# Seven products of block sums for the FFN up projection, and a down projection in parts

## The chip, the cores and the metric

The kernel runs on one core of one Trainium2 chip. The metric is the device time of one execution in microseconds (us); lower is better. Engines are named as in the profile: PE (TensorE, matmul) with PEld (its weight loads), DVE (VectorE), ACT (ScalarE), POOL (GpSimd) and SP (the queue that issues most transfers).

## The reference

The input x is 512 tokens by 1024 features in float32. Two layers follow each other: a token mixer (gated linear attention in layer 0, grouped-query softmax attention in layer 1) and, after each, a gated MLP, the FFN, which this change is about:

```python
def conv_ffn(h, w_up, w_conv, b_conv, w_down):
    u = h @ w_up                       # (512, 1024) @ (1024, 5632)
    u = depthwise_conv_width3(u, w_conv) + b_conv
    val, gate = jnp.split(u, 2, axis=-1)
    return (jax.nn.silu(gate) * val) @ w_down    # (512, 2816) @ (2816, 1024)

x = x + conv_ffn(rmsnorm(x, norm_ffn[i]), ...)
```

The 2816 hidden features are 22 chunks of 128. A chunk has a value half and a gate half, each 128 features wide.

## The kernel before

**Data.** Everything lies feature by token: x is eight tiles of 128 features by 512 tokens (`x[c]`). Each float32 operand of a projection is used as two float32r pieces, high and low, and a product is three matmuls: high by high, high by low, low by high (`mm3`, lines 268 to 272).

**Weights.** The class `Weights` (line 103) keeps a list `todo` of half tiles of 128 by 1024 in the order of use. `make` loads a raw tile of 1 MB on the SP queue into one of two buffers, and makes the high piece on ACT and the low piece on DVE (`split`, lines 143 and 144), into one of three `wh` and `wl` buffers each. For a few attention weights (`by_dma`) the low piece is made without DVE: ACT writes the negated high piece (line 124), and a transfer issued by POOL adds the raw weights to it (line 133, issued at the next `flush`). `half` hands out one half and makes the next one ahead.

**FFN** (`ffn`, line 588). For each of the 22 chunks, two feature tiles (value and gate) of 8 times `mm3` with 512 tokens as moving columns go into a PSUM bank each: 48 matmuls. The input of these matmuls is x times the norm's weight. The token factor R of the norm comes later: the sum of squares is turned into R by matmuls and copies beside chunk 0 (`tokens`, `rows`, line 266), and DVE multiplies the PSUM result by R (line 605). Then the width-3 convolution on ACT and DVE (lines 607 to 609), SiLU, product and split into high and low (lines 611 to 615) give `gu`, the down projection's input. All 22 `gu` are kept. After the last chunk, the down projection runs over the eight feature tiles of the output: 22 times `mm3` into one bank, one DVE addition to x (line 633), then the pieces and squares for the next norm (`chunk`).

**Order.** The program's text gives each instruction its rank, and a planner at compile time orders each engine's queue by rank among what it reckons to be ready. An engine then works its queue strictly in that order. Tiles share buffers by tag; a new tile waits until an earlier holder's last reader is done. The tag `g` has 22 buffers of 4 KB per partition (`gu` and much else), `xhl` has 8 (the norm's pieces).

## Time and profile before

| what | value |
|---|---|
| median of 3 timed runs | 1135.24 us |
| lowest and highest | 1134.88 and 1135.59 us |
| profiled execution | span of 1132.5 us from the first to the last instruction; the page gives no time around it, and the median lies 2.74 us above the span |
| PE, share of the span | 99% busy |
| DVE | 60% |
| ACT | 42% |
| POOL | 8% |
| FFN of layer 0 | from 231 to 592 us |
| FFN of layer 1 | from 768 to 1129 us |

A busy time of one matmul is longer than the distance to the next one, since matmuls are pipelined; the cost of a run of matmuls is therefore read from the distance of their starts. A line number is that of the kernel before, and a helper's line stands for all its callers, so tiles are named with it (`up` and `dn` are the PSUM banks of the up and down projection, `av` and `po` those of two attention steps).

### The profile page before, as it was taken

The numbers are of one execution on the slowest core, as the hardware profiler recorded it, in microseconds if no ns is written. First come the engines' busy times: TensorE is split into PE (matmuls) and PEld (weight loads), VectorE is DVE, ScalarE is ACT, GpSimd is POOL, SyncE is SP. The second block draws the span as 40 slices with busy tenths as digits, with TensorE's granted clock in tenths as the row PEclk, the third lists the DMA queues.
The fourth block names the chain that finished last, engine by engine and source line by source line (L and its number), as shares of the span: only waits on it lengthen the run. The fifth ranks groups of instructions, "written<-read, shape, count | busy, mean of one in ns | idle before, by whom it ended". The sixth has DMA issues, their size and how long they took to land. (4 is left out here: it accounts for less than half of the span.)

```text
span 1132.5 us, 13117 instructions
## 1 busy us (share of the span) xinstructions
PE 1124.2 (99%) x5266; PEld 937.4 (83%) x5266; DVE 683.7 (60%) x989; ACT 481.2 (42%) x690; POOL 86.2 (8%) x74
## 2 busy tenths in 40 slices
PE   9999999999999999999999999999999999999998
PEld 7878888888888888888888888888888888888887
DVE  6576654577777777633325688766777677762221
ACT  5555233444444444422234667644444444442210
POOL 0214110000000000000004343000000000000000
PEclk9999999999999999999999999999999999999999
DMA  6322221222323223233247765423232232323320
GB/s 230 121 100 77 75 75 38 75 98 89 112 75 112 95 91 112 76 110 106 81 132 194 182 171 158 150 75 112 75 112 80 107 111 76 111 84 121 130 93 19
DMA packets 24589, 120.06 MB, mean 106 GB/s; under 512 B 2896, under 2 KB 3536, under 8 KB 13008
## 3 DMA queue, kind: packets, MB, share of 16 engines
q1 hardware_dynamic: 17328, 102.29, 26.0%
q0 software_dynamic: 2304, 8.39, 3.9%
q10 hardware_dynamic: 4896, 8.54, 2.1%
q8 instruction: 41, 0.67, 0.2%
q14 instruction: 20, 0.16, 0.0%
HBM read 100.34 MB, written 2.10 MB: 90 GB/s over the span
## 5 line engine op out<-in xcount | busy, mean ns | idle before, releaser
L143 ACT ACTIVATE wh<-raw 128x1024 fp32r<-128x1024 f32 x164 | 172.9, 1055 | 338.0 <-PE up L271 132.8
L144 DVE TENSOR_TENSOR wl<-raw,wh 128x1024 fp32r<-128x1024 f32 x164 | 203.8, 1243 | 142.7 <-ACT wh L143 142.3
L270 PE MATMUL up<-xhl,wh 128*128 128x512 f32 x704 | 274.3, 390 | 0.0
L272 PE MATMUL up<-xhl,wl 128*128 128x512 f32 x704 | 273.9, 389 | 0.0
L271 PE MATMUL up<-xhl,wh 128*128 128x512 f32 x704 | 273.9, 389 | 0.0
L271 PEld LDWEIGHTS up<-xhl,wh 128*128 128x128 f32 x704 | 132.2, 188 | 27.6
L272 PEld LDWEIGHTS up<-xhl,wl 128*128 128x128 f32 x704 | 132.1, 188 | 27.4
L270 PEld LDWEIGHTS up<-xhl,wh 128*128 128x128 f32 x704 | 132.1, 188 | 27.2
L271 PE MATMUL dn<-gu,wh 128*128 128x512 f32 x354 | 137.3, 388 | 0.0
L272 PE MATMUL dn<-gu,wl 128*128 128x512 f32 x354 | 137.3, 388 | 0.0
L270 PE MATMUL dn<-gu,wh 128*128 128x512 f32 x354 | 137.3, 388 | 0.0
L605 DVE TENSOR_TENSOR u<-up,R 128x512 f32<-128x512 f32 x88 | 60.3, 687 | 52.7 <-PE up L272 52.7
L299 PE MATMUL vg<-wh,xhl 128*128 128x512 f32 x256 | 80.1, 391 | 1.5 <-DVE halfneg L188 0.7
L607 ACT ACTIVATE y<-u,cw 128x512 f32<-128x512 f32 x88 | 71.1, 811 | 20.4 <-DVE u L605 20.4
L270 PEld LDWEIGHTS dn<-gu,wh 128*128 128x128 f32 x354 | 66.5, 188 | 13.8
L271 PEld LDWEIGHTS dn<-gu,wh 128*128 128x128 f32 x354 | 66.5, 188 | 13.7
L272 PEld LDWEIGHTS dn<-gu,wl 128*128 128x128 f32 x354 | 66.5, 188 | 13.5
L325 PE MATMUL op<-oT,wh 128*128 128x512 f32 x256 | 71.1, 394 | 0.3 <-DVE oT L710 0.3
L609 DVE SCALAR_TENSOR_TENSOR y<-u,cw,y 128x511 f32<-128x511 f32 x88 | 65.9, 751 | 2.9
L608 DVE SCALAR_TENSOR_TENSOR y<-u,cw,y 128x511 f32<-128x511 f32 x88 | 65.6, 746 | 0.6 <-ACT y L607 0.6
L611 ACT ACTIVATE y<-y 128x512 f32<-128x512 f32 x44 | 27.9, 633 | 87.8 <-DVE y L609 87.8
L299 PEld LDWEIGHTS vg<-wh,xhl 128*128 128x128 f32 x256 | 48.0, 188 | 12.4 <-DVE g L368 1.0
(187 smaller groups left out, 1432.3 us busy)
## 6 DMA issues: line engine op xcount, KB each, us to landing
raw<-in_w_up_dram SPq DMA_DIRECT2D x44, 1024.0 KB, 4.8
raw<-in_w_down_dram SPq DMA_DIRECT2D x22, 1024.0 KB, 4.8
wl<-raw POOLq DMA_DIRECT2D x16, 512.0 KB, 4.8
pr<-p ACTq DMA_DIRECT2D x32, 256.0 KB, 3.1
raw<-in_w_vg_dram SPq DMA_DIRECT2D x6, 1024.0 KB, 4.8
raw<-in_w_akq_dram SPq DMA_DIRECT2D x5, 1024.0 KB, 5.3
raw<-in_w_kq_dram SPq DMA_DIRECT2D x4, 1024.0 KB, 4.7
raw<-in_w_gout_dram SPq DMA_DIRECT2D x4, 1024.0 KB, 4.8
```

What stands on the lines that cost most here:

```text
L143: act.activation(hi[:, sl], r[:, sl], AF.Copy)
L144: dve.tensor_tensor(lo[:, sl], r[:, sl], hi[:, sl].bitcast(F32), ALU.subtract)
L270: mm(ps, wh, mh, start=start, stop=False)
L271: mm(ps, wh, ml, start=False, stop=False)
L272: mm(ps, wl, mh, start=False, stop=stop)
L299: mm(ps[j][:, :width], hl[k][i == 2][:, js[j]], (wl if i == 1 else wh)[:, sl], start=k == 0 and i == 0, stop=k == KC - 1 and i == 2)
L325: mm(pss[ng][n], wt[:, sl], mv, start=k == 0 and i == 0, stop=k == KC - 1 and i == 2)
L605: dve.tensor_tensor(u, ps, norm.R, ALU.mult)
L607: act.activation(y, u, AF.Identity, scale=w(1), bias=w(3))
L608: dve.scalar_tensor_tensor(y[:, 1:], u[:, : S - 1], w(0), y[:, 1:], ALU.mult, ALU.add)
L609: dve.scalar_tensor_tensor(y[:, : S - 1], u[:, 1:], w(2), y[:, : S - 1], ALU.mult, ALU.add)
L611: act.activation(res[1], res[1], AF.Silu)
```

## The change

**Seven products.** Chunks 0 to 3 stay as they are, and are called plain here. For chunks 4 to 21 of both layers the chunk's weights are seen as 2 by 2 blocks: rows are the value half and the gate half, columns are the first and second 512 input features (A11, A12; A21, A22). The input is seen as 2 by 2 blocks as well: rows are the feature halves, columns the token halves of 256 (B11, B12; B21, B22). The 2 by 2 block product is formed from seven products of block sums in place of eight plain ones. Each product is 4 times `mm3` with 256 moving columns, so 12 matmuls, and a chunk has 84 of them. The gate rows are used with the opposite sign, which three convolution taps per gate feature, negated once, take back.

**Input forms.** The seven forms of the input (B11, B21, B22 and the sums T1 to T4) have the token factor R in them already. They are made once a layer, spread over plain chunks 1 to 3 (`build`): 8 scaled copies of x, 4 sums on DVE or POOL in halves, 7 splits on ACT and DVE. They hold 14 of the 22 `g` buffers through the layer.

**Weight sums.** `load` fetches the raw tile, and A21 once more into a tile `e`; two accumulating transfers issued by POOL add A22 to `e` and A11 to the raw tile's A21. `sum12` and `sum43` add on DVE and split, `rowA1` and `oneA22` only split. Down weights come as half tiles of 512 KB into `xhl` buffers and get their low piece by the accumulating transfer, as do the weights of the plain chunks. Once the plain chunks are through, up to four keys are made ahead (`AHEAD`) in place of one.

**Down projection in parts.** The chunks form six parts of 4, 4, 4, 4, 3 and 3. The down tiles of a part (eight output tiles over that part's chunks) run beside the next part's chunks, two or three tiles in each (`TILES`), after the fourth of the seven products; each adds its bank to x. The tiles of the last part follow the last chunk.

**Buffers.** Work tiles of the mixers and the FFN move into pools of their own, opened and closed by stage. The FFN has four tiles `w4` of 1024 columns (u and y of a chunk) and two `v`.

The function `gated` holds lines 604 to 616 of before on tiles that have both halves side by side.

```diff
@@ -36,6 +37,11 @@
+PLAIN = 4
+PARTS = (4, 4, 4, 4, 3, 3)
+TILES = {4: (2, 2, 2, 2), 3: (3, 3, 2)}
+AHEAD = 4
@@ -103,34 +112,90 @@
     class Weights:
...
         def make(self, key):
+            if isinstance(key[0], str):
+                getattr(self, key[0])(key)
+                return
             src, i, h = key
+            alone = any(src is a for a in down)
+            if alone:
+                first = src is down[0] and False
+                t = pair("xhl", 8, F32, "draw") if (i, h) != (0, 0) else big(F32, "draw")
+                sync.dma_start(t, src[i][:, h * 2 * S : (h + 1) * 2 * S])
+                self.convert(key, t, (i, h) == (0, 0), True)
+                return
...
+        def convert(self, key, r, spare, by_dma):
+            n = r.shape[1]
+            if spare:
+                hi, lo = (pair("xhl", 8, F32R, n_)[:, :n] for n_ in ("xwh", "xwl"))
+            else:
+                hi, lo = pair("wh", 3, F32R, "wh")[:, :n], pair("wl", 3, F32R, "wl")[:, :n]
+            act.activation(hi, r, AF.Copy)
+            if by_dma:
                 act.activation(lo, r, AF.Copy, scale=-1.0)
-                self.pending.append((lo, r))
+                self.pending.append((lo.bitcast(F32), r))
             else:
-                self.split(hi, lo, r, 2 if src is w_vg and i < 2 else 1, src is w_vg and i == 0 and h == 0)
-            self.made[id(src), i, h] = (hi, lo)
+                dve.tensor_tensor(lo, r, hi.bitcast(F32), ALU.subtract)
...
+        def load(self, key):
+            _, layer, m = key
+            src = up[layer][m]
+            r = sp.tile([P, 4 * S], F32, tag="raw", bufs=2, name=nm("raw"))
+            e = big(F32, "sum") if m <= PLAIN + 1 else pair("xhl", 8, F32, "sum")
+            sync.dma_start(r, src)
+            sync.dma_start(e[:, :S], src[:, 2 * S : 3 * S])
+            self.pending.append((e[:, :S], src[:, 3 * S :]))
+            self.pending.append((r[:, 2 * S : 3 * S], src[:, :S]))
+            self.raw[layer, m], self.sums[layer, m] = r, e
+        def rowA1(self, key):
+            _, layer, m = key
+            self.convert(key, self.raw[layer, m][:, : 2 * S], m > PLAIN, False)
+        def sum12(self, key):
+            _, layer, m = key
+            r, e = self.raw[layer, m], self.sums[layer, m]
+            dve.tensor_tensor(e[:, S:], e[:, :S], r[:, :S], ALU.add)
+            self.convert(key, e, m > PLAIN, False)
+        def sum43(self, key):
+            _, layer, m = key
+            r, e = self.raw[layer, m], self.sums[layer, m]
+            dve.tensor_tensor(r[:, S : 2 * S], r[:, S : 2 * S], e[:, S:], ALU.add)
+            self.convert(key, r[:, S : 3 * S], False, False)
+        def oneA22(self, key):
+            _, layer, m = key
+            self.convert(key, self.raw.pop((layer, m))[:, 3 * S :], m == PLAIN, False)
+            del self.sums[layer, m]
         def flush(self):
-            for lo, r in self.pending:
-                pool.dma_start(lo.bitcast(F32), r, accum_op=ALU.add)
+            for dst, src in self.pending:
+                pool.dma_start(dst, src, accum_op=ALU.add)
             self.pending = []
...
+        def get(self, key):
             self.flush()
             while key not in self.made:
                 self.make(self.todo.pop(0))
-            if self.todo:
+            while self.todo and len(self.made) <= self.ahead:
                 self.make(self.todo.pop(0))
             return self.made.pop(key)
...
+    def part_tiles(p):
+        first = KC * sum(PARTS[:p])
+        return [(c, range(first + c * PARTS[p], first + (c + 1) * PARTS[p])) for c in range(KC)]
+    def part_keys(layer, tiles):
+        return [(down[layer], u // 16, u // 8 % 2) for _, us in tiles for u in us if u % 8 == 0]
+    def schedule():
+        beside, m = {}, 0
+        for p, n in enumerate(PARTS):
+            tiles = part_tiles(p - 1) if p else []
+            for share in TILES[n]:
+                beside[m], tiles, m = tiles[:share], tiles[share:], m + 1
+        return beside
+    BESIDE = schedule()
+    def add_ffn(layer):
+        for m in range(PLAIN):
+            if m == PLAIN - 1:
+                W.todo.append(("load", layer, PLAIN))
+            W.todo += [(up[layer], m, 0), (up[layer], m, 1)]
+        for m in range(PLAIN, FC):
+            if m + 1 < FC:
+                W.todo.append(("load", layer, m + 1))
+            W.todo += [(n, layer, m) for n in ("rowA1", "sum12", "sum43")]
+            W.todo += part_keys(layer, BESIDE[m])
+            W.todo.append(("oneA22", layer, m))
+        W.todo += part_keys(layer, part_tiles(len(PARTS) - 1))
...
-    W.by_dma += [(a, 1) for a in qk_order + [w_av]] + [(w_aout, 2)]
+    add_ffn(1)
+    W.by_dma += [(a, 1) for a in qk_order + [w_av]] + [(w_aout, 2)] + [(a, PLAIN) for a in up]
...
@@ -576,6 +678,10 @@
+        taps = cw.rearrange("p (l t m w) -> p l t m w", l=2, t=2, m=FC)
+        for l in range(2):
+            v_ = taps[:, l, 1, PLAIN:, 0:3]
+            dve.tensor_scalar(v_, v_, -1.0, None, ALU.mult)
@@ -586,60 +692,181 @@
     def ffn(layer, norm, cw, nxt):
...
+        H = S // 2
+        wide = lambda n: stage[-1].tile([P, 2 * S], F32, tag="w4", bufs=4, name=nm(n))
+        hl, forms = [], {}
+        def build():
+            hs = []
+            for i in range(4):
+                t = big(F32, "h")
+                for e in range(2):
+                    c = 2 * i + e
+                    dve.scalar_tensor_tensor(t[:, e * S : (e + 1) * S], x[c], norm.weight(c), norm.R,
+                                             ALU.mult, ALU.mult)
+                    yield
+                hs.append(t.rearrange("p (c s) -> p c s", s=S))
+            q2 = (slice(0, 2), slice(2, 4))
+            blk = lambda i, j: [hs[2 * i + q][:, :, j * H : (j + 1) * H] for q in range(2)]
+            b11, b12, b21, b22 = blk(0, 0), blk(0, 1), blk(1, 0), blk(1, 1)
+            v4 = lambda t: t.rearrange("p (k s) -> p k s", s=H)
+            def pieces(name, srcs):
+                hi, lo = v4(big(F32R, "th")), v4(big(F32R, "tl"))
+                n = 4 // len(srcs)
+                for q, src in enumerate(srcs):
+                    sl = slice(q * n, (q + 1) * n)
+                    act.activation(hi[:, sl], src, AF.Copy)
+                    dve.tensor_tensor(lo[:, sl], src, hi[:, sl].bitcast(F32), ALU.subtract)
+                forms[name] = (hi, lo)
+            def combine(eng, dst, a, b, op):
+                for q in range(2):
+                    eng.tensor_tensor(dst[:, q2[q]], a[q], b[q], op)
+            halves = lambda t: [t[:, q] for q in q2]
+            pieces("B11", b11)
+            yield
+            t1, t2, t3 = (v4(big(F32, "ts")) for _ in range(3))
+            combine(dve, t1, b11, b12, ALU.subtract)
+            yield
+            combine(dve, t2, b22, halves(t1), ALU.add)
+            yield
+            pieces("T2", [t2])
+            yield
+            pieces("T1", [t1])
+            yield
+            combine(pool, t3, b22, b12, ALU.subtract)
+            combine(pool, t2, halves(t2), b21, ALU.subtract)
+            yield
+            pieces("B21", b21)
+            yield
+            pieces("B22", b22)
+            yield
+            pieces("T3", [t3])
+            yield
+            pieces("T4", [t2])
+            yield
+        building = build()
+        def gated(m, u):
+            y = wide("y")
+            for t in range(2):
...
+                act.activation(yt, ut, AF.Identity, scale=w(1), bias=w(3))
+                dve.scalar_tensor_tensor(yt[:, 1:], ut[:, : S - 1], w(0), yt[:, 1:], ALU.mult, ALU.add)
+                dve.scalar_tensor_tensor(yt[:, : S - 1], ut[:, 1:], w(2), yt[:, : S - 1], ALU.mult, ALU.add)
+            act.activation(y[:, S:], y[:, S:], AF.Silu)
+            dve.tensor_tensor(y[:, :S], y[:, :S], y[:, S:], ALU.mult)
+            t = big(F32R, "gu")
+            act.activation(t[:, :S], y[:, :S], AF.Copy)
+            dve.tensor_tensor(t[:, S:], y[:, :S], t[:, :S].bitcast(F32), ALU.subtract)
+            hl.append((t[:, :S], t[:, S:]))
+        def plain(m):
+            u = wide("u")
             for t in range(2):
                 ps = bank("s" if t else "acc", "up")
                 feature_tile(*W.half(up[layer], 2 * m + t), norm.hl, ps)
...
                 if m == 0 and t == 0:
                     norm.tokens()
                 elif m == 0:
                     norm.rows()
...
+                else:
+                    for _ in range(4 if m < PLAIN - 1 else 8):
+                        next(building, None)
...
+            gated(m, u)
+        def product(dst, pair_, at, form, start, stop):
+            hi, lo = forms[form]
+            for kk in range(4):
+                sl = slice((at + kk) * P, (at + kk + 1) * P)
+                for i, (w, b) in enumerate(((pair_[0], hi), (pair_[0], lo), (pair_[1], hi))):
+                    mm(dst, w[:, sl], b[:, kk], start=start and kk == 0 and i == 0,
+                       stop=stop and kk == 3 and i == 2, skip_group_check=True)
+        cur = [None]
+        def down_tile(p, c, us, last):
             ps = bank("acc", "dn")
...
+            k0 = sum(PARTS[:p])
+            late = []
+            for i, u in enumerate(us):
                 if u % 8 == 0:
...
+                    cur[0] = W.half(down[layer], u // 8)
                 sl = slice((u % 8) * P, (u % 8 + 1) * P)
...
+                mm3(ps, cur[0][0][:, sl], cur[0][1][:, sl], *hl[k0 + i], i == 0, i == len(us) - 1)
...
+            dve.tensor_tensor(x[c], x[c], ps, ALU.add)
+            if last and nxt is not None:
+                nxt.chunk(c)
+            elif last:
+                sync.dma_start(out[c * P : (c + 1) * P, :], x[c])
+        def seven(m, part):
+            X = bank("s", "X")
+            a1 = W.get(("rowA1", layer, m))
+            product(X[:, :H], a1, 0, "B11", True, False)
+            s12 = W.get(("sum12", layer, m))
+            product(X[:, H:], s12, 4, "T2", False, True)
+            v = stage[-1].tile([P, H], F32, tag="v", bufs=2, name=nm("v"))
+            act.activation(v, X[:, :H], AF.Copy)
+            dve.tensor_tensor(v, v, X[:, H:], ALU.subtract)
+            Y = bank("pt", "Y")
+            product(Y[:, :H], s12, 0, "T1", True, False)
+            s43 = W.get(("sum43", layer, m))
+            product(Y[:, H:], s43, 4, "T3", False, False)
+            u = wide("u")
+            dve.tensor_tensor(u[:, 3 * H :], v, Y[:, :H], ALU.add)
+            dve.tensor_tensor(u[:, 3 * H :], u[:, 3 * H :], Y[:, H:], ALU.add)
+            for c, us in BESIDE[m]:
+                down_tile(part - 1, c, us, False)
+            product(X[:, :H], a1, 4, "B21", False, True)
+            act.activation(u[:, :H], X[:, :H], AF.Copy)
+            a22 = W.get(("oneA22", layer, m))
+            product(Y[:, H:], a22, 0, "T4", False, True)
+            product(Y[:, :H], s43, 0, "B22", False, True)
+            dve.tensor_tensor(u[:, H : 3 * H].rearrange("p (t s) -> p t s", s=H),
+                              v.rearrange("p (t s) -> p t s", t=1).to_broadcast([P, 2, H]),
+                              Y.rearrange("p (t s) -> p t s", s=H), ALU.add)
+            gated(m, u)
+        m = 0
+        for part, n in enumerate(PARTS):
+            for _ in range(n):
+                if m < PLAIN:
+                    plain(m)
+                    if m == PLAIN - 1:
+                        for _ in building:
+                            pass
+                        W.ahead = AHEAD
+                else:
+                    seven(m, part)
+                m += 1
+        W.ahead = 1
+        for c, us in part_tiles(len(PARTS) - 1):
+            down_tile(len(PARTS) - 1, c, us, True)
...
@@ -925,7 +1165,9 @@
-    dn = dn.transpose(0, 3, 1, 2, 4).reshape(2, KC * FC // 16, 16, P, P)
+    ends = np.cumsum((0,) + PARTS)
+    dn = np.concatenate([dn[:, a:b].transpose(0, 3, 1, 2, 4).reshape(2, -1, P, P) for a, b in zip(ends, ends[1:])], axis=1)
+    dn = dn.reshape(2, KC * FC // 16, 16, P, P)
```

More of the change, by code (lines that the diff above doesn't have):

```diff
@@ L107, in __init__ @@
         def __init__(self):
-            self.todo, self.made, self.raw, self.by_dma, self.pending = [], {}, {}, [], []
+            self.todo, self.made, self.raw, self.sums, self.by_dma, self.pending = [], {}, {}, {}, [], []
+            self.ahead = 1
         def add(self, src):
@@ L179, in hybrid_encoder_kernel @@
     ident = identr.bitcast(F32)
-    two = tmp("u", "two")
+    two = tmp("sq", "two")
     dve.memset(two[:, :P], 2.0 ** -5)
```

101 lines of the change are left out of this document (48 added, 53 removed).

## The prediction

> **What bounds the kernel now.** I began with the page's head, the first part (busy time by engine) and the chain of waits.
>
> ```profile
> span 1132.5 us, 13117 instructions
> PE 1124.2 (99%) x5266; PEld 937.4 (83%) x5266; DVE 683.7 (60%) x989; ACT 481.2 (42%) x690; POOL 86.2 (8%) x74
> PE 38%; DVE 1%; issue 0%; ACT 0%; ACTq 0%; DVEq 0%
> raw<-in_w_up_dram SPq DMA_DIRECT2D x44, 1024.0 KB, 4.8
> ```
>
> PE never rests, and only PE and a trace of DVE carry shares in the chain. So the time moves by what PE issues, plus any new idle time of PE. The sum is made against the span and carried to the median of the timed runs, 1135.24 us, as a difference: the 2.7 us around the span have no part in the change. Less than 0.2% (2.3 us) counts as no change.
>
> Next the timeline of PE, for the distance of matmul starts: an up tile of layer 0 with 512 columns, then the attention steps `av` and `po`, the nearest with 256, and their counts from the view of line 299.
>
> ```profile
> 440.21 0.39 PE L270 MATMUL up<-xhl,wh 128*128 128x512 f32 x1
> ...
> 445.65 0.39 PE L270 MATMUL up<-xhl,wh 128*128 128x512 f32 x1
> ```
>
> ```profile
> L299 PE MATMUL av<-wh,xhl x64: 281/283/283, 616.6 to 628.0; 128*128 128x256 f32 x64
> L299 PE MATMUL av<-wl,xhl x32: 283/283/283, 616.7 to 627.8; 128*128 128x256 f32 x32
> L299 PEld LDWEIGHTS av<-wl,xhl x32: 187/192/192, 616.6 to 627.7; 128*128 128x128 f32 x32
> 616.55 0.28 PE L299 MATMUL av<-wh,xhl 128*128 128x256 f32 x1
> ...
> 628.07 0.40 PE L270 MATMUL s<-k,q 128*128 128x512 f32 x1
> 739.47 0.28 PE L270 MATMUL po<-pth,vh 128*128 128x256 f32 x1
> ...
> 740.90 0.40 PE L325 MATMUL op<-oT,wh 128*128 128x512 f32 x1
> ```
>
> With 512 columns 24 matmuls take 5.44 us, 0.2267 each. With 256, the 96 of `av` take 11.52 us, 0.1200 each, and the 12 of `po` 1.43 us, 0.1192 each. Half the columns cost 53% of the time, and a weight load of 0.19 us does not set this pace.
>
> **The change part by part.**
>
> *PE.* A chunk takes 48 × 0.2267 = 10.88 us now. Seven products take 84 × 0.1192 = 10.01 us by `po`, 84 × 0.1200 = 10.08 us by `av`; I take the middle, 10.05. The gain is 0.83 us on each of 36 chunks: **-29.9 us**, between -28.8 and -31.3. One eighth of the columns goes, but a good third of it is lost to the shorter matmul. The down projection keeps its 1056 matmuls, at no change.
>
> [...]
>
> *DVE beside it.* Rows of two chunks of layer 0 from the timeline of DVE and ACT, then groups by line and shape:
>
> ```profile
> 417.97 0.69 DVE L605 TENSOR_TENSOR u<-up,R 128x512 f32<-128x512 f32 x1 [1.31 <-PE up L272]
> 418.71 0.81 ACT L607 ACTIVATE y<-u,cw 128x512 f32<-128x512 f32 x1
> 418.83 1.23 DVE L144 TENSOR_TENSOR wl<-raw,wh 128x1024 fp32r<-128x1024 f32 x1 [0.17 <-ACT wh L143]
> 419.98 0.74 DVE L608 SCALAR_TENSOR_TENSOR y<-u,cw,y 128x511 f32<-128x511 f32 x1
> 420.76 0.75 DVE L609 SCALAR_TENSOR_TENSOR y<-u,cw,y 128x511 f32<-128x511 f32 x1
> 422.26 0.69 DVE L612 TENSOR_TENSOR y<-y,y 128x512 f32<-128x512 f32 x1 [0.76 <-ACT y L611]
> 423.66 0.69 DVE L615 TENSOR_TENSOR gu<-y,gu 128x512 fp32r<-128x512 f32 x1 [0.70 <-ACT gu L614]
> 424.27 0.69 DVE L605 TENSOR_TENSOR u<-up,R 128x512 f32<-128x512 f32 x1
> 424.87 1.22 DVE L144 TENSOR_TENSOR wl<-raw,wh 128x1024 fp32r<-128x1024 f32 x1
> 426.00 0.74 DVE L608 SCALAR_TENSOR_TENSOR y<-u,cw,y 128x511 f32<-128x511 f32 x1
> ```
>
> ```profile
> L144 DVE TENSOR_TENSOR wl<-raw,wh 128x1024 fp32r<-128x1024 f32 x164 | 203.8, 1243 | 142.7 <-ACT wh L143 142.3
> L143 ACT ACTIVATE wh<-raw 128x1024 fp32r<-128x1024 f32 x164 | 172.9, 1055 | 338.0 <-PE up L271 132.8 <-PE dn L271 127.5 <-PE op L325 34.1
> L443 DVE TENSOR_TENSOR ga<-ga,t 128x256 f32<-128x256 f32 x8 | 3.3, 418 | 0.0
> L614 ACT ACTIVATE gu<-y 128x512 fp32r<-128x512 f32 x44 | 27.8, 633 | 33.0 <-DVE y L612 33.0
> L527 ACT ACTIVATE sa<-kv 128x256 f32<-128x256 f32 x8 | 3.1, 384 | 8.3 <-PE kv L526 8.3
> ```
>
> Per changed chunk DVE has three low pieces of 1024 (3.73 us), one of 512 and two weight additions (2.07), assembly of u with three operations of 256 and one of 512 (1.94), four convolution steps (3.0), product and split (1.38), and two additions to x (1.38): 13.5 us, before it was 8.2. ACT has 3.80 us of high pieces, 0.77 of PSUM copies, 2.89 in `gated` and 2.11 for a down half: 9.6. PE has 10.05 plus two down tiles of 12 matmuls, 5.44: 15.5 us. So the conversions, the assembly and the 80 extra additions to x cost nothing while they stay behind PE; DVE fills 87% of that cover, against 76% before. Without the cover the 13.5 would bound, which is a rival.
>
> *Entry into the changed chunks.* The forms need R.
>
> ```profile
> 768.13 0.39 PE L270 MATMUL up<-xhl,wh 128*128 128x512 f32 x1
> 780.60 0.69 DVE L266 COPY R<-bc 128x512 f32<-128x512 f32 x1 [3.36 <-PE bc L211]
> ```
>
> R stands 13.2 us after layer 1's first up matmul. Four plain chunks and the norm's own matmuls end about 44.9 us after it, so DVE has 31.7 us. By distances of starts above (0.61 us for 512 elements, 0.78 for a convolution step, 1.13 for 1024) it owes by then: `gated` and u of three chunks, 16.6; eight scaled copies of x, 6.2; sums, 2.4; low pieces of the forms, 8.2; the first weight row and half of the next u, 1.7: 35.1 us, so 3.4 late. Next late is `sum12` of chunk 4, ranked behind these: addition, ACT's split and the low piece add 2.8. PE has one product (1.43 us) to hide this: 3.4 + 2.8 - 1.4 = 4.8 idle, less where the planner slips `sum12` into a gap. I take 4 per layer, **+8 us**, between 0 and 16.
>
> *End of each layer.* The last part's first output tile needs `gu` of chunk 21. By the rows from 417.97 to the end of L615 at 424.35, u to low piece takes 6.4 us with only the gate half to do; without the wedged weight operation (0.4) and with two more convolution steps for the value half it is 7.5, and 6.8 to the high piece. Three PSUM banks let PE run 18 matmuls of older chunks meanwhile, 4.1 us; in strict order it is 6, 1.4 us. Idle 2.7 to 5.4 a layer, where before it was hidden behind 21 chunks; I take 3, **+6 us** (5.4 to 10.8).
>
> *Part boundaries.* Four times a layer the same chain stands against 48 products' matmuls and nine of a down tile, 5.7 + 2.0 = 7.8 us. With one weight operation wedged in, the high piece comes at about 8: **+2 us** (0 to 6).
>
> *Late low pieces of down weights.* For a half, ACT writes both pieces, then POOL issues the accumulating transfer; rows from the end of layer 0, and the spread from the view of tile `wl`:
>
> ```profile
> 586.44 1.06 ACT L123 ACTIVATE wh<-raw 128x1024 fp32r<-128x1024 f32 x1 [3.44 <-PE dn L271]
> 588.75 0.87 POOL L133 DMA_DIRECT2D wl<-raw  x1 [4.38 <-ACT wl L124]
> DMA to landing us min/median/max: 4.5/4.8/8.7
> ```
>
> From ACT's start to landing it is 2.3 + 4.8 = 7.1 us. Of three `wh` buffers one is kept through the chunk by `sum43`, one goes to the next `sum43`, and the third comes free when T4's product ends, 1.43 us before the chunk's end. So the piece lands 5.7 us into the next chunk; the first down tile's third matmul needs it at 6.2. In time by 0.5 us, and B21, T4 and B22 can fill in if the planner foresees a delay. I take **+2 us**. Behind this transfer on POOL wait the two weight sums of the chunk after next, which have a chunk's time to spare; the raw load on SP waits in turn for the raw buffer, which `oneA22` frees early in the chunk. The traffic per chunk, 1.75 MB of up and 1 MB of down, is 2.8 MB in 15.5 us or 180 GB/s; the chip moved 230 in the page's first slice:
>
> ```profile
> GB/s 230 121 100 77 75 75 38 75 98 89 112 75 112 95 91 112 76 110 106 81 132 194 182 171 158 150 75 112 75 112 80 107 111 76 111 84 121 130 93 19
> ```
>
> *Into attention.* An output tile now takes PE 2.04 us; addition, low piece and square sum take DVE 2.0. A small lag remains: **+0.5 us**. Pools by stage and negated taps (two DVE operations): 0.
>
> The sum: -29.9 + 8 + 6 + 2 + 2 + 0.5 = -11.4, so 1135.2 - 11.4 = **1124 us**.
>
> **The rivals.**
>
> *All but the layer's end is hidden.* PE is never short and the planner fills every gap: -31.3 + 5.4 = -25.9, **1109 us**. For it speaks that PE is 99% busy through all stages of the kernel before; against it R's late arrival.
>
> *A wash.* Every idle term at its upper end: -28.8 + 16 + 10.8 + 6 = +4 at most, about 1136.
>
> *DVE's queue becomes the bound (slower).* In the rows above DVE idles 1.31 + 0.17 + 0.76 + 0.70 = 2.9 us in a chunk, most of it on ACT inside `gated`. If the new work doesn't fill these holes, a chunk lasts 13.5 + 2.9 = 16.4 us against PE's 15.5. It decides from 13.5 + 2.0 on. Price 0.95 × 36 = +34; with the gain, the layer's end and the entry to attention, +11: **1146 us**. Against it: the planner places ready weight work in such holes.
>
> *The down half's low piece lands late (slower).* If ACT takes it up 1.5 us later, one conversion and a copy, PE waits 1.0 us in each chunk: 36 - 13.4 = +23, **1158 us**. It decides from 0.4 us of waiting per chunk. [...]
>
> *Weight loads set the pace.* If the load's 0.19 us bounded the short matmul, 84 × 0.19 = 16.0 us, +5.1 × 36 = +183: **1318 us**. The 0.12 us of `av` and `po` speak against it. [...]
>
> **How the numbers follow.** Forecast 0.45 (its own range 1113 to 1132), all hidden 0.24, wash 0.08, DVE's queue 0.12, late low piece 0.09, loads 0.02. Faster 0.69, same 0.08, slower 0.23. The range runs from 1108, just under the full gain, to 1150, past DVE's bound; the late piece and the loads are left out.
>
> **What would show it.** Products' starts 0.119 to 0.120 us apart confirm the first term; above 0.125 the gain is below 15 us. PE idle about 4 us before chunk 4's T2 product, released by `sum12` on DVE, and about 3 before the first tile of the last part, released by `gu`, confirm those. PE waiting for DVE in every chunk with DVE over 95% busy means the third rival; PE waiting for POOL's transfer at the down tiles the fourth. A new idle time elsewhere, above all in the mixers, would make the prediction wrong.

## The result and the profile after

The changed kernel takes **1354.25 us** (median of four runs, 1351.96 to 1358.77) against 1135.06 (1134.16 to 1135.59) for the kernel before on the same chip: a ratio of 1.194, 95% interval 1.1914 to 1.1965. The prediction was 1124 us, range 1108 to 1150: wrong in sign. The profiled execution took 1358.77 us, its span is 1357.1.

First the page of the kernel after: busy time, the slices of PE's granted clock, the two groups with most idle time ahead of them, and the DMA issues.

```profile
span 1357.1 us, 16954 instructions
PE 1178.2 (87%) x6562; PEld 1023.1 (75%) x6562; DVE 820.4 (60%) x1271; ACT 625.5 (46%) x914; POOL 215.2 (16%) x214
PEclk9999999979788888898989999998888888789999
...
L374 PE MATMUL dn<-gu,wl 128*128 128x512 f32 (+1 forms) x338 | 158.8, 472 | 134.3 <-DMA wl<-draw 134.2
L159 DVE TENSOR_TENSOR xwl<-raw,xwh 128x1024 fp32r<-128x1024 f32 (+1 forms) x36 | 43.0, 1194 | 168.1 <-DMA wl<-draw 160.4
...
raw<-in_w_up_dram SPq DMA_DIRECT2D x44, 1024.0 KB, 8.3
wl<-draw POOLq DMA_DIRECT2D x42, 512.0 KB, 9.5
wl<-raw POOLq DMA_DIRECT2D x32, 512.0 KB, 5.0
```

Two things changed beside the count of matmuls. PE idles 1357.1 - 1178.2 = 178.9 us, before 8.3: **+170.6**. And PE is busy 54.0 us longer where 29.9 fewer were due: **+84 us** are matmuls that took longer. The slices of the granted clock show most of why: in slices 9 to 21 and 28 to 36, inside the two FFNs, it is 7 to 9 tenths. By the trace's record of the granted clock (the clock record from here on) PE works 142.8 us at half speed, so 71 of the 84 us are the clock; the other 13 are not resolved. The balance is 170.6 - 29.9 + 83.9 = 224.6, the whole difference of the spans (1357.1 - 1132.5). The group of L374 names the wait: the matmul with the low piece `wl` of a down half waits for the accumulating transfer `wl<-draw`, 134 of the 170.6 us. That transfer lands 9.5 us after its issue; the same kind of transfer for weights of attention and of plain chunks, where hardly any weight sums run, lands after 5.0.

The view of waits of the kernel after, all engines and then PE alone (us in total, times, longest):

```profile
DVE xwl L159 <- DMA wl<-draw: 160.4, 22, 8.6
...
PE dn L374 <- DMA wl<-draw: 134.2, 27, 6.9
PE dn L372 <- ACT gu L767: 10.6, 6, 2.4
PE X L796 <- DVE wl L159: 8.5, 2, 4.5
PE up L372 <- ACT wh L154: 6.0, 2, 3.4
...
PE up L374 <- DMA wl<-raw: 3.8, 2, 2.4
```

Now one chunk of layer 0 in the timeline (start, duration, engine, operation, idle time before it and its releaser):

```profile
437.78 0.80 PE L374 MATMUL dn<-gu,wl 128*128 128x512 f32 x1 [5.44 <-DMA wl<-draw]
...
445.37 0.28 PE L796 MATMUL X<-th,xwh 128*128 128x256 f32 x1
...
448.33 1.06 ACT L154 ACTIVATE wh<-draw 128x1024 fp32r<-128x1024 f32 x1
449.69 0.28 PE L796 MATMUL X<-th,xwh 128*128 128x256 f32 x1
450.33 0.86 POOL L198 DMA_DIRECT2D sum<-in_w_up_dram  x1 [11.46 <-PE Y L796]
450.87 1.22 POOL L198 DMA_DIRECT2D wl<-draw  x1
451.60 0.33 SPq L168 DMA_DIRECT2D raw<-in_w_up_dram  x1
...
455.45 0.40 PE L372 MATMUL dn<-gu,wh 128*128 128x512 f32 x1
...
462.13 1.23 DVE L159 TENSOR_TENSOR xwl<-raw,xwh 128x1024 fp32r<-128x1024 f32 x1 [7.76 <-DMA wl<-draw]
462.15 0.80 PE L374 MATMUL dn<-gu,wl 128*128 128x512 f32 x1 [6.07 <-DMA wl<-draw]
```

84 product matmuls run from 445.37 to 455.45, 0.120 us apart: that part is as predicted. The block is the last three products of one chunk (up to 449.69) and the first four of the next, in the order of the program's text. The two down tiles follow behind it, so nothing is left to fill a wait in them. ACT starts on the down half at 448.33, 1.36 us before the chunk's end, where the prediction had 1.43. POOL issues the transfer at 450.87, and it lands at 462.1: **13.8 us after ACT's start**, 11.2 after the issue. Beside it go a transfer for a weight sum (450.33) and the next chunk's raw megabyte (451.60). The first down tile's third matmul is there at about 456.1, 6.4 us into the chunk (6.2 in the prediction), and waits 6.07 us. DVE waits for the same transfer, 7.76 us: the low piece of the next chunk's first row goes into a buffer of the tag `xhl`, which the `draw` tile holds until the transfer has read it. From one such wait to the next, 437.78 to 462.15, are 24.4 us, not 15.5.

After the wait the matmuls are slow. The view of stretches of the kernel after (us, then busy time and count of PE, PEld, DVE, ACT, POOL, then granted clock, DMA share, GB/s):

```profile
437.70:443.00 5.30, 5.22 (x12) 4.13 (x13) 5.24 (x9) 0.63 (x1) 0.86 (x1) 0.50 0.29 49
445.30:455.40 10.10, 10.10 (x86) 10.06 (x85) 6.07 (x8) 8.02 (x11) 1.76 (x2) 1.00 0.41 86
455.40:462.10 6.70, 0.68 (x4) 0.24 (x2) 0.00 (x0) 0.26 (x1) 0.00 (x0) 0.86 0.71 185
```

For 5.3 us after the wait the granted clock is 0.50 and only 12 matmuls start; then it is 1.00. And in the 6.7 us of the next wait the DMA engines are 71% busy with 185 GB/s, close to the 180 that the prediction worked out as the mean of a chunk and held to be harmless.

### The profile page after: what moved, and what is told of

Read it like the earlier page. It is cut to its first block, busy times and chain, and to the rows that moved or that the text cites. A ratio compares the mean times of both kernels' runs of the same rounds, so it can differ in the third digit from the quotient of the medians.

```text
span 1357.1 us, 16954 instructions
## 1 busy us (share of the span) xinstructions
PE 1178.2 (87%) x6562; PEld 1023.1 (75%) x6562; DVE 820.4 (60%) x1271; ACT 625.5 (46%) x914; POOL 215.2 (16%) x214
## 5 line engine op out<-in xcount | busy, mean ns | idle before, releaser
L374 PE MATMUL dn<-gu,wl 128*128 128x512 f32 (+1 forms) x338 | 158.8, 472 | 134.3 <-DMA wl<-draw 134.2
L374 PEld LDWEIGHTS dn<-gu,wl 128*128 128x128 f32 x338 | 78.1, 231 | 164.0 <-DMA wl<-draw 146.5
L372 PE MATMUL dn<-gu,wh 128*128 128x512 f32 (+1 forms) x338 | 154.3, 462 | 10.6 <-ACT gu L767 10.6
L373 PE MATMUL dn<-gu,wh 128*128 128x512 f32 (+1 forms) x338 | 152.5, 451 | 4.1 <-DVE gu L768 4.1
L796 PE MATMUL Y<-th,wl 128*128 128x256 f32 x432 | 123.0, 285 | 0.0
L796 PE MATMUL Y<-th,wh 128*128 128x256 f32 x432 | 123.0, 285 | 0.0
L796 PE MATMUL Y<-tl,wh 128*128 128x256 f32 x432 | 122.9, 285 | 0.0
L796 PE MATMUL X<-th,xwl 128*128 128x256 f32 x408 | 115.5, 283 | 0.0
L796 PE MATMUL X<-tl,xwh 128*128 128x256 f32 x408 | 115.5, 283 | 0.0
L796 PE MATMUL X<-th,xwh 128*128 128x256 f32 x408 | 115.3, 283 | 0.0
L159 DVE TENSOR_TENSOR wl<-raw,wh 128x1024 fp32r<-128x1024 f32 x72 | 69.8, 972 | 26.5 <-ACT wh L154 26.5
L796 PEld LDWEIGHTS Y<-th,wl 128*128 128x128 f32 x432 | 83.9, 194 | 0.0
```

Of the source, the lines that this page charges most:

```text
L159: dve.tensor_tensor(lo, r, hi.bitcast(F32), ALU.subtract)
L372: mm(ps, wh, mh, start=start, stop=False)
L373: mm(ps, wh, ml, start=False, stop=False)
L374: mm(ps, wl, mh, start=False, stop=stop)
L796: mm(dst, w[:, sl], b[:, kk], start=start and kk == 0 and i == 0, stop=stop and kk == 3 and i == 2, skip_group_check=True)
```

## The experiments

My theory after these views had two parts: the low piece is late because it shares the DMA engines with the transfers for the sums and the raw load, and each wait also costs clock. Rivals: the transfer is simply started too late; the short dense matmuls themselves bring the clock down; DVE's queue would bound the kernel anyway.

**The down half's low piece on DVE.**

```diff
-                self.convert(key, t, (i, h) == (0, 0), True)
+                self.convert(key, t, (i, h) == (0, 0), False)
```

> The low piece of each down half is made by DVE (lo = raw - hi) in place of ACT's second activation and POOL's accumulating transfer; all else as in the changed kernel. Theory A (the transfer of that piece lands late, PE idles some 6 us in each changed chunk, and the clock then restarts at half speed for some 5 us): the waits for that transfer go, the granted clock returns to above 0.98, and the time falls from 1354 to between 1115 and 1150 us; DVE has 14.7 us of work per chunk of 15.5, so it may show waits of its own. Theory B (the clock falls because of the dense 256-column matmuls, whatever PE waits for): the clock in the FFN stays below 0.95 and the time above 1180. Theory C (all transfers are late because the DMA engines are overloaded): the waits pass to the weight sums, 1200 to 1300 us.

Measured: 1160.04 us (1156.99 to 1161.58; before 1134.5), ratio 1.0215, interval 1.0194 to 1.0237. The page, the stretch 850 to 1000 us, and PE's waits of this kernel:

```profile
span 1159.9 us, 16788 instructions
PE 1119.7 (97%) x6562; PEld 989.1 (85%) x6562; DVE 862.2 (74%) x1315; ACT 590.6 (51%) x870; POOL 176.4 (15%) x170
```

```profile
850.00:1000.00 150.00, 150.00 (x1035) 139.89 (x1034) 128.03 (x182) 78.65 (x106) 16.40 (x19) 1.00 0.58 157
```

```profile
PE dn L372 <- ACT gu L767: 12.7, 6, 3.2
PE X L796 <- DVE wl L159: 8.2, 2, 4.3
PE up L372 <- ACT wh L154: 5.8, 2, 3.4
```

One word takes away 194 of the 219 us. In the stretch PE never rests: 1035 matmuls at 84 + 24 a chunk are 9.58 chunks, 15.65 us each, at clock 1.00. So dense short matmuls do not bring the clock down, and DVE, with 85% of the stretch, does not bound it. Yet the kernel is 25 us slower than before. By spans: idle time 40.2 against 8.3, +31.9; the gain -29.9; and PE busy only 4.5 us less than before, so 25.4 more in longer matmuls: +27.4 together. Of these 25.4 us the clock record explains 18 (36.5 us of PE at half speed). The idle time is the layer's entry, the part boundaries and the layer's end.

**Down halves made ahead of `sum43`**, so that the transfer starts earlier and away from the others.

```diff
-            W.todo += [(n, layer, m) for n in ("rowA1", "sum12", "sum43")]
+            W.todo += [(n, layer, m) for n in ("rowA1", "sum12")]
             W.todo += part_keys(layer, BESIDE[m])
+            W.todo.append(("sum43", layer, m))
```

> Only the order of the keys changes: the down half stands ahead of sum43, so it gets the weight buffer that comes free when the down tiles end, 2.9 us earlier than T4's end. Theory A with a plain late start: the wait per chunk shrinks by about 3 of 6 us, the time is near 1354 - 36 x 3 - some clock = 1220 to 1260 us, and the transfer still takes 9 to 10 us to land. Theory A with a collision (the transfer takes 9.5 us instead of 4.8 because it starts together with the 1 MB raw load of a later chunk): started earlier it lands in 5 to 7 us, and the time falls to 1130 to 1180. Theory C: no change, 1330 to 1360.

Measured: 1272.41 us (one run). Its page, PE's waits, and ACT's start on one half:

```profile
raw<-in_w_up_dram SPq DMA_DIRECT2D x44, 1024.0 KB, 5.0
...
wl<-draw POOLq DMA_DIRECT2D x42, 512.0 KB, 5.5
```

```profile
PE dn L375 <- DMA wl<-draw: 65.4, 32, 3.7
```

```profile
507.10 1.06 ACT L154 ACTIVATE wh<-draw 128x1024 fp32r<-128x1024 f32 x1 [3.17 <-DMA draw<-in_w_down_dram]
```

The same transfer lands after 5.5 us instead of 9.5, the raw load after 5.0 instead of 8.3, and the raw load is now issued 5.2 us behind the transfer, not 0.7: the collision is real. PE still waits 2.0 us at each of 32 places, for a reason of this kernel's own. ACT starts only when the raw half has landed, in the chunk of the row above 1.2 us after the chunk's end; in the kernel after it started 1.36 us before it. So a late start explains what is left here, and not the wait of the kernel after.

**The sums without transfers**: A21 is not loaded twice, and DVE makes both additions.

```diff
-            sync.dma_start(e[:, :S], src[:, 2 * S : 3 * S])
-            self.pending.append((e[:, :S], src[:, 3 * S :]))
-            self.pending.append((r[:, 2 * S : 3 * S], src[:, :S]))
...
+            dve.tensor_tensor(e[:, :S], r[:, 2 * S : 3 * S], r[:, 3 * S :], ALU.add)
+            dve.tensor_tensor(r[:, 2 * S : 3 * S], r[:, 2 * S : 3 * S], r[:, :S], ALU.add)
```

> The two weight sums that POOL's accumulating transfers make (A21+A22, A21+A11) and the second load of A21 are left to DVE, two more additions of 512 per chunk (1.2 us, 14.9 us in all); the low piece of the down half still comes by transfer. If the sums' transfers are what the down half's transfer collides with or queues behind on POOL: it lands in 5 to 7 us and the time falls to 1150 to 1230. If the raw load of 1 MB alone is the collision: landing stays at 8 to 10 us, 1320 to 1370 us. If DVE's queue is near its bound: waits for DVE appear on PE, above 1354.

Measured: 1191.8 us (one run). PE's waits:

```profile
PE X L795 <- ACT wh L154: 20.2, 2, 10.5
...
PE dn L373 <- DMA wl<-draw: 9.7, 9, 3.2
```

Untouched itself, the transfer lands after 5.4 us by the page's median, and PE's wait for it falls from 134.2 to 9.7. The raw load still goes beside it, issued 1.3 us behind it in the chunk at 449 us. So neither of the two holds it up alone: without the sums it lands after 5.4 us beside a raw load, and with the sums, but the raw load issued later, after 5.5. The kernel after shows the same: its 22 transfers with a raw load issued within 1.2 us of theirs, a sum beside them as well, land after 9.3 to 12.0 us, and the other 20 after 4.5 to 6.9, several beside a sum. Whether the transfers hold each other up in a queue or on the DMA engines, no run separates. A new wait of 10 us a layer for `wh` appears at the entry; its cause was not followed up.

**Both on DVE.** The last two edits together.

> Both repairs at once: the low pieces of down weights and the two weight sums are made by DVE, so the changed chunks have no accumulating transfer at all. DVE then has 13.5 + 1.2 + 1.2 = 15.9 us per chunk by busy means (14.6 by distances of starts) against PE's 15.5. If DVE's work counts by the distances of starts it still fits: 1150 to 1170 us, near the kernel with the low pieces alone on DVE (1160). If it counts by busy means or if the holes of its queue stay open (the prediction's third rival, 2.9 us per chunk), PE waits for DVE in each chunk: 1180 to 1250 us.

Measured: 1162.2 us (one run), PE 96% and DVE 78% busy. DVE takes the additions too without becoming the bound; what is left is mostly the entry (20.8 us of PE waiting for `wh` from ACT).

**The parts alone**: all 22 chunks plain, the down projection still in six parts, low pieces on DVE.

```diff
-            W.todo += [(n, layer, m) for n in ("rowA1", "sum12", "sum43")]
+            W.todo += [(up[layer], m, 0), (up[layer], m, 1)]
...
-                    seven(m, part)
+                    plain(m)
+                    for c, us in BESIDE[m]:
+                        down_tile(part - 1, c, us, False)
```

> One part of the change alone: all 22 chunks are plain (eight block products as one, weights split by ACT and DVE as before), and the down projection runs in six parts with its tiles after the chunks of the next part; low pieces of down weights by DVE. The prediction's terms for the layer's end (2.7 us idle each layer) and part boundaries: 1135 + 5 to 10 = 1140 to 1145 us, clock 0.99 or more. Rival: the parts themselves (80 more additions to x, three or four matmul groups per bank, weights of up and down in turns) cost much, 1160 us or more.

Measured: 1147.17 us (1145.9 to 1147.31), ratio 1.0108, interval 1.0093 to 1.0124: **+12.7 us** with none of the products. Its page and PE's longest wait:

```profile
span 1145.4 us, 13309 instructions
PE 1129.7 (99%) x5266; PEld 937.0 (82%) x5266; DVE 734.4 (64%) x1069; ACT 480.5 (42%) x690; POOL 86.5 (8%) x74
```

```profile
PE dn L367 <- ACT wh L154: 5.4, 5, 1.6
```

With the same 5266 matmuls as before, PE is busy 5.5 us longer and idles 7.4 longer. Only 1.6 of the 5.5 are half speed by the clock record; the rest stays open. The idle time lies near the 8 us that the prediction gave boundaries and layer ends together, but that is luck: here PE waits for the down weights' high pieces from ACT, and not once for `gu`. So this run shows what the parts cost beside plain chunks, and does not test those two terms.

**The entry.** On top of the low piece on DVE: the first two plain chunks get their low pieces by DVE, the last input sums go from POOL to DVE, and the first `sum12` is made early. Then, on top of that, a down tile of the last chunk placed behind its products.

```diff
-            if any(src is a and i < n for a, n in self.by_dma):
+            if any(src is a and i < n for a, n in self.by_dma) and not (i < 2 and any(src is a for a in up)):
...
-            combine(pool, t3, b22, b12, ALU.subtract)
-            combine(pool, t2, halves(t2), b21, ALU.subtract)
+            combine(dve, t3, b22, b12, ALU.subtract)
+            combine(dve, t2, halves(t2), b21, ALU.subtract)
...
+                    if m == PLAIN - 1 and t == 1:
+                        W.make(W.todo.pop(0))
```

> The kernel with down low pieces on DVE (1160), and three edits at the entry into the changed chunks: weights of plain chunks 0 and 1 get their low piece from DVE in place of the transfer, the two input sums of POOL go to DVE, and sum12 of chunk 4 is ranked ahead of the last input forms. Theory: of the 25 us that separate it from the kernel before, the entry holds about 19 us of idle (5.8 in plain chunks, where ACT waits for a raw tile whose buffer the transfer holds; 9.7 at chunk 4's first sum), plus a restart at half clock after each gap, some 2.4 us each. If the edits close most of these gaps: 1135 to 1148 us, clock 0.985 or more. If DVE is simply too full before chunk 4, the gap moves and the time stays at 1152 to 1165.

> The entry edits, and one of the last chunk's two down tiles moved behind its seven products, as cover for gu of chunk 21. Theory: the gap of 3.2 + 1.2 us at the end of each layer shrinks by the tile's 2.0 us of matmuls, and with under 2 us left the restart at half clock (2.4 us) may be spared too: 4 to 9 us less than the kernel with the entry edits alone. If the gap isn't what counts there: the same time within 2 us.

Measured: 1155.44 us (1153.33 to 1156.04), ratio 1.0175 (1.016 to 1.019), and 1153.91 (1151.18 to 1157.77), ratio 1.0169 (1.0141 to 1.0198). The wait for `sum12` falls from 3.9 to 1.75 us in layer 0, but waits of 2.1 and 2.5 us for another piece of DVE (`v`) come up at the entry, and those of the plain chunks stay almost as they were. The gap at the layer's end goes from 3.2 to 3.05 only. The tile does stand behind the products, so PE has 27 matmuls ahead of the gap in place of 18; but `gu` comes 1.9 us later after the last product, since DVE takes up one more addition to x and one more low piece ahead of its last convolution steps (layer 0 of the second kernel):

```profile
581.54 0.68 DVE L823 TENSOR_TENSOR x<-x,dn 128x512 f32<-128x512 f32 x1
582.14 1.22 DVE L159 TENSOR_TENSOR wl<-draw,wh 128x1024 fp32r<-128x1024 f32 x1
```

The reason for moving the sums to DVE was in the timeline of the kernel with the low piece on DVE:

```profile
275.17 3.88 POOL L726 TENSOR_TENSOR ts<-ts,h 128x512 f32<-128x512 f32 x2 [1.21 <-DVE tl L721]
277.83 1.77 DVE L762 SCALAR_TENSOR_TENSOR y<-u,cw,y 128x511 f32<-128x511 f32 x1
...
279.52 5.14 DVE L721 TENSOR_TENSOR tl<-h,th 128x512 fp32r<-128x512 f32 x4
```

With the sums on DVE the same four splits take half as long:

```profile
275.50 2.49 DVE L721 TENSOR_TENSOR tl<-h,th 128x512 fp32r<-128x512 f32 x4
```

One by one, the two of the four that run beside an addition on POOL take 1.77 and 2.23 us, the other two 0.68 each. A convolution step takes 1.77, not 0.74. The prediction priced the POOL sums at nothing for DVE. Why DVE is slower beside them, no run shows.

**Five plain chunks**, for a longer entry (parts 5, 4, 4, 3, 3, 3), with the tile at the layer's end held by an ordering edge.

> Built on the kernel with the entry and end edits (1154): five plain chunks instead of four (parts of 5, 4, 4, 3, 3, 3), so DVE has 10.9 us more before the first changed chunk, and the last chunk's second down tile is held behind its last product by an ordering edge, which the planner had pulled forward. Theory: what is left of the loss is idle at the entry (9 us in layer 0, 12 in layer 1) and at the layer's end (4 us each), each gap followed by a restart at half clock. One more plain chunk costs 0.8 us of gain a layer, and should close 5 us or more of entry gaps and one or two restarts a layer; the tile should take 2 us and a restart: 1125 to 1142 us, which would be level with or ahead of the kernel before. If the entry gaps come from buffers (raw tiles, `wh`) and not from DVE's load, they move one chunk later and the time stays at 1148 to 1158.

Measured: 1176.46 us (1174.34 to 1180.22), ratio 1.036 (1.0338 to 1.0383): worse. PE's waits of this kernel:

```profile
PE dn L372 <- ACT gu L767: 16.2, 10, 3.0
PE X L798 <- ACT wh L154: 11.9, 2, 7.1
PE up L374 <- DMA wl<-raw: 8.1, 4, 2.3
```

A further chunk of time does not help. The waits for `gu` at boundaries and layer ends grow from 10.2 us in six places to 16.2 in ten, and at the entry those for `wh` and for transfers grow; I took the latter for pieces whose raw buffer a transfer still holds. The ordering edge changes nothing at the layer's end, a gap of 3.04 us. So the next pair makes all plain low pieces on DVE, with four and with five plain chunks.

```diff
-    W.by_dma += [(a, 1) for a in qk_order + [w_av]] + [(w_aout, 2)] + [(a, PLAIN) for a in up]
+    W.by_dma += [(a, 1) for a in qk_order + [w_av]] + [(w_aout, 2)]
```

> Four plain chunks, the entry and end edits, the second down tile of the last chunk held behind the last product, and now all weights of the plain chunks get their low piece from DVE: the FFN has no accumulating transfer but those of the weight sums. Buffer theory (the five-plain-chunk kernel's long waits for ACT's `wh` and for the transfer `wl<-raw` at the entry come from transfers that hold a raw tile while the next load waits for its buffer): these waits vanish, DVE is 4.5 us fuller before chunk 4, and the time falls from 1154 to 1140 to 1150 us. DVE theory (the entry is bound by DVE's work before chunk 4): DVE's extra 4.5 us a layer appear as idle PE time, 1156 to 1170 us.

> The same with five plain chunks, so that DVE has 10.9 us more against 7.8 us more of work. Buffer theory: the entry gaps of 17 and 15 us in the two layers of the kernel with five plain chunks (1176) shrink to under 6 us, 1130 to 1145 us. If the raw tiles and the three `wh` buffers are held by something else than the transfers, the wait for ACT at the first changed chunk stays, 1160 to 1180 us.

Measured with four: 1150.16 us (six runs, 1144.21 to 1152.24), ratio 1.0139 (1.012 to 1.0157). PE's waits:

```profile
PE X L798 <- DVE wl L159: 10.5, 4, 5.2
```

With five: 1162.36 us (1161.12 to 1168.64), ratio 1.0248 (1.0214 to 1.0282). Its waits:

```profile
PE dn L372 <- ACT gu L767: 22.1, 10, 3.3
PE up L374 <- DVE wl L209: 9.2, 2, 4.7
```

In both the waits for transfers are gone, and DVE is late in their place, by as much as 5.2 us: the buffers and DVE's load each hold back the entry when the other is relieved. With five plain chunks the entry's gaps are under 6 us, as the buffer theory said, but its time is not: `gu` is now the largest wait, and why it is later there stays open. No version with the seven products beats the kernel before; the best is the one with four plain chunks, 15 us slower.

**What an idle time costs.** In the kernel before, PE is made to wait after chunks 3, 6, 9, 12, 15 and 18 for a chain of 1, 3, 6, 10, 15 and 24 small ACT operations; nothing of the change is in it.

```diff
+            if m in GAPS:
+                q = tmp("sq", "gap", P)
+                dve.tensor_copy(q, pss[1][:, :P])
+                for _ in range(GAPS[m]):
+                    act.activation(q, q, AF.Copy, scale=0.5)
+                gb = bank("po", "gap")
+                gate = mm(gb[:, :8], q, q[:, :8], start=True, stop=True)
```

> The kernel before, with nothing of the change: after chunks 3, 6, 9, 12, 15 and 18 of each layer a small matmul has to wait for a chain of 1, 3, 6, 10, 15 and 24 ACT operations that begins when the chunk's last matmul ends, and the next chunk's matmuls are held behind it. So PE idles for six lengths, about 1 to 8 us, in a stream of 512-column matmuls. Idle theory (any idle stretch of PE past some length between 1 and 3 us is followed by about 5 us at half clock, 2.4 us lost, whatever ran before): starts 0.43 us apart after the longer gaps and none after the shortest, a mean clock of 0.97 to 0.985, and the time some 40 us of gaps plus 15 to 25 us of slow clock above 1135. Rival (the slow clock belongs to the short matmuls or to the transfers of the changed kernel): no slow starts after any gap, clock 0.998 or more, 1170 to 1180 us.

Measured: 1219.56 us against 1136.39. The waits of PE, the stretches behind the first two gaps of layer 0 (1.12 us, up to 277.32; 2.37 us, up to 312.84), and the stretch behind the second gap of layer 1 (2.37 us as well, up to 894.08):

```profile
PE gap L610 <- ACT gap L608: 59.0, 12, 10.3
```

```profile
277.50:280.00 2.50, 2.50 (x13) 2.09 (x14) 2.24 (x3) 0.61 (x2) 0.00 (x0) 1.00 0.03 10
313.20:316.00 2.80, 2.80 (x9) 2.22 (x9) 1.50 (x3) 1.17 (x2) 0.00 (x0) 0.50 0.00 0
316.20:319.00 2.80, 2.80 (x14) 2.29 (x14) 0.62 (x1) 0.00 (x0) 0.00 (x0) 1.00 0.00 0
894.30:897.30 3.00, 3.00 (x15) 2.49 (x15) 1.65 (x3) 1.22 (x2) 0.00 (x0) 1.00 0.00 0
```

After 1.12 us of idling the clock stays at 1.00 in both layers. After 2.37 us it is 0.50 for 3.2 us in layer 0, and stays at 1.00 in layer 1. After the four longer gaps it is 0.50 for 3.2 to 6.4 us in either layer, with matmuls 0.43 us apart. The span grew by 83.2 us against the kernel before on the same chip (1217.8 - 1134.6), of which 59.0 are the gaps themselves. Of the other 24.2 the clock record explains 21.9 (PE works 43.7 us at half speed) behind nine gaps: **2.4 us each**. The theory's "past some length" is too simple: what a gap between some 1.3 and 3.4 us costs is not settled by its length. Over all 13 traces half speed followed each of the 50 idle times of PE of 3.4 us or more (26 of them in the kernel after, 3.42 to 6.92 us), 48 of the 74 from 2 to 3.4, 10 of the 49 from 1.3 to 2, and one of the 46 from 0.8 to 1.3. The idling alone brings the clock down, in a stream of 512-column matmuls: a mean of 0.972 over the span, against 1.000 in the kernel before. What besides its length decides whether a gap of 2.37 us slows PE, no run shows.

## Why the prediction was wrong

- **PE, -29.9: right.** 84 matmuls in 10.08 us in the kernel after, and 15.65 us per chunk against 15.5 in the kernel with the low piece on DVE.
- **Late low pieces of down weights, +2: the step that failed.** "From ACT's start to landing it is 2.3 + 4.8 = 7.1 us", in time by 0.5. It was 13.8 in the chunk shown. All else in that step came as predicted: ACT's start 1.36 us before the chunk's end, POOL's issue 2.5 us later, the need 6.4 us into the next chunk. The term that failed is the landing: the 4.8 is the median of accumulating transfers in a kernel whose FFN has none of its own; under the change's own traffic it is 9.5, and 9.3 to 12.0 where a sum and a raw load go beside it. The remedies show it: without the transfer -194 us, without the sums beside it -162, with the raw load out of its way -82. The rival of the late low piece had place and sign right but another cause, a later start on ACT; it had 1.0 us a chunk and 9 in 100, and the range left it out. The row quoted for the 4.8 had 8.7 as its maximum, and that alone would have made it 3.4 us late.
- **"B21, T4 and B22 can fill in": wrong.** The planner kept the order of the text in every changed chunk: the down tiles stand in one block, and these three products behind it wait with them, 6.07 us in the chunk shown.
- **DVE held by the same transfer: not foreseen.** The `draw` tile shares the `xhl` buffers with the next row's low piece; DVE waits 160 us in total. No view shows PE waiting for those low pieces behind the entry, so what this costs stays open.
- **The bandwidth, "180 GB/s; the chip moved 230": wrong use of a mean.** Transfers of a chunk bunch, 185 GB/s beside a DMA share of 71% during PE's wait; what matters is the landing of the one that PE waits for.
- **The clock: no term for it.** By the clock record 71 us in the kernel after, and 18 in the kernel with the low piece on DVE, where the gaps are those that the prediction did list. In the latter a gap costs a restart on top at the entry, at both layer ends (a wait of 3.23 us, then matmuls 0.42 to 0.43 us apart) and at one boundary (2.22 us), but not at the boundaries with 1.84 and 1.66.
- **Entry, +8: right for `sum12`, incomplete.** In the kernel after PE waits 8.5 us in two places for the low piece on DVE, 4 to 4.5 a layer, as stated. The size is in part luck: DVE loses some 4.8 us in layer 0 to the sums on POOL, which were priced at nothing for it. And the plain chunks ahead idle too, 6.0 for high pieces on ACT and 3.8 for accumulating transfers: 18.3 in all where 8 were priced, two shorter waits (2.9) and the restarts beside.
- **Layer end +6: right as idle time. Boundaries +2: too low.** In the kernel with the low piece on DVE PE waits 12.7 us for `gu` in six places: 3.23 at each layer's end, 6.5 together, and 6.2 at the boundaries, the upper end of their range. The restarts come on top. The parts alone cost 12.7 us too, but by other waits and by longer busy time, for which there was no term.
- **Rivals.** DVE's queue as the bound: refuted, PE is 100% busy beside a DVE of 85%. Weight loads: refuted by 0.120 us. A wash and all hidden: even with the late piece mended the kernel is 25 us slower than before. (The wash's +4 gives 1139, not 1136.)

What stays open is how the entry would have to be arranged: whether raw buffers, `wh` buffers or DVE's load is first in line changed from run to run, and a version with more buffers was not tried. Open too are the 13 us of longer matmuls in the kernel after, 7 in the one with the low piece on DVE, that the clock does not explain.

## What to carry to other kernels

Price a transfer on the critical path by its landing beside the traffic that the change itself adds, and look for who else waits for the buffer that it reads; a median from a quiet kernel was half the price here, 4.8 against 9.5 us. Count a new idle time of PE as its length plus a restart where one like it was slowed in these traces (all 50 of 3.4 us or more, 48 of 74 from 2 to 3.4); in the run with gaps a restart cost 2.4 us. Where a saving is 0.8 us per chunk, a handful of such gaps per layer (entry, part boundaries, end) is enough to lose all of it.

## What the hardware showed that was not expected

- In the run with gaps, the granted clock was 0.50 for 3.2 us after PE had idled 2.37 us in one layer, and 1.00 after the same in the other; after 1.12 us it was 1.00 in both, after 3.39 to 10.3 us 0.50 in both.
- In the kernel after, an accumulating transfer of 512 KB landed after 4.5 to 6.9 us where no raw load of 1 MB was issued within 1.2 us of it, even beside an accumulating one of 256 KB, and after 9.3 to 12.0 with both beside it. With a raw load alone, issued 1.3 us behind it in the kernel without the sums' transfers, it took 5.4 at the median.
- In the kernel after, matmuls of 256 columns stay 0.120 us apart through a chunk's 84, with a weight load each: 86 matmuls beside 85 loads in 10.1 us, at a granted clock of 1.00.
- In the kernel with the low piece on DVE, two subtractions of 128x512 on DVE that ran beside an addition on POOL took 1.77 and 2.23 us, and 0.68 each the two of the same four that did not.
